# One streaming-encoder layer on one core: norm and weight loads given out a piece ahead of their squares, gate sigmoids a slot behind their loads

## The chip, the cores and the metric

The kernel runs on one core of a Trainium2 chip. The metric is the device time of one execution in microseconds; lower is better. Of the kernel before, three runs and one profiled execution are at hand.

## The reference, cut to what matters

One layer of an encoder for 2048 new frames (16 tiles of 128 rows) and for 8 running streams of 16 frames each (one more tile, number 16, called NT). Two mixers run side by side: differential attention (4 heads) and stick-breaking attention (8 heads of 64, taken in pairs). Their outputs are gated and merged.

```python
h = rms_norm(x, norm_g) * (1.0 + scale) + shift
qa, ka, va, za, qb, kb, vb, zb, ga, gb = split(h @ w_in)
...
s = einsum('bqhcd,bkhcd->bhcqk', qa, ka) * HEAD_DIM_A ** -0.5        # chunk-causal mask
p = softmax(s);  w = p[:, :, 0] - lam * p[:, :, 1];  oa = w @ va
...
z = einsum('bqhd,bkhd->bhqk', qb, kb) * HEAD_DIM_B ** -0.5
log_a = log_sigmoid(z) + cumsum(log_1m, reverse=True) - log_1m;  ob = exp(log_a) @ vb
...
oa = rms_norm(oa, subln_g) * (1.0 - lam_init)
ya = (oa * silu(za)) @ w_branch_a
yb = (ob * silu(zb)) @ w_branch_b
x = x + gate * ((sigmoid(ga) * ya + sigmoid(gb) * yb) @ w_out)
y = rms_norm(x, final_g)
```

The running streams attend to a cache of 512 past frames each (cache_a_k, cache_a_v, cache_b_k, cache_b_v) beside their own frames. Keys and values are returned too.

## The kernel before, in words

Every matmul operand is split in two float16 parts (a high part and what it leaves, three products per matmul), after a scaling by a power of two. The power follows from a bound: the sum of the squares of the weights or cache rows. So each piece of weights and of cache is loaded, squared and summed on ScalarE (`sum_squares`, line 281 is its instruction), and scaled and split later on (`split`, lines 299 to 304).

The program has three stages. In the first (to about 70 us) the modulated inputs are made and stored. The second runs eight units, one head or pair of heads each: even units are differential attention, odd ones stick-breaking. A unit walks over the 17 tiles; `steps` is the list of the 136 pairs of unit and tile. A step projects a tile (lines 438 and 514, running about five tiles ahead), computes scores (lines 649 to 653), turns them into weights on VectorE, ScalarE and GpSimd, has them transposed by DMA (`turn`, line 590, tile wt) and multiplies them with the values two steps later (lines 706 to 711).

Three kinds of side work are dealt out over the steps as lists of small functions called pieces, at the head of each step:

- `prepare_unit` makes the next unit's weights: four pieces `norm` (a load and its square), one `bounds`, four pieces `cut` (the split); odd units the same once more for the gates' weights.
- `norms` returns two lists. `spare` has 48 pieces `one`: a load and its square, for the branch weights, w_out and the cached values. `cached` has 34 pieces `stages` for the 32 pieces of cached keys: a piece splits and stores one, squares the next and loads the one after that.
- The pace is set by the loop over steps: so many pieces per step that a list is through by its due step.

All of these take their 4 KB buffers (wa, wb) from one list, `free`: the front is popped, what is done with is appended. Loads and stores are issued from SyncE's queue (`load` is `nc.sync.dma_start`). Within the engines' queues a scheduler sets the order from the order in which the program is written and from what depends on what.

The third stage (from about 1820 us) is the last phase. Slot n does the branch matmuls of tile n (`branches`, line 1366), the output matmuls of tile n−1 (`output`, line 1395), the rows of tile n−2 (`normed_rows`), and `inputs` of tile n+2: its loads of o, z and the gates' rows (g_d, line 1222), the sigmoid of z, the gates' sigmoids, a sum of squares and the split (line 299, tile hs). `turned` transposes the split tile on TensorE (line 1209). Beside them runs the lane of the cached streams (`sample`, tiles dsc, v16c, dks). Four gate buffers serve two tiles in turn. `act` (line 123) is the helper through which sigmoids and exponentials go, in an order that is kept.

Of the kernel before, what the change touches and what calls it, by code (L numbers as in the profile page):

```python
# [20 lines left out]
AF = mybir.ActivationFunctionType  # L21
# [4 lines left out]
P = 128  # L26
D = 1024
KT = D // P
# [85 lines left out]
def layer_kernel(ctx: ExitStack, tc: tile.TileContext, a: dict):  # L114
# [201 lines left out]
    def prepare_unit(u, keep=None):  # L316


        h, kind = u // 2, u % 2
        U = dict(h=h, kind=kind, u=u, w=[], wg=[], bufs=[])  # L320
        units[u] = U
        raw = {}
        g0, gw = GATES[u]
        gk = 1024 // gw if gw else 0

        def fetch(name, k):
            raw[name, k] = b = free.pop(0) if keep is None else keep[:, k // 2, :]
            if name == "w":
                st = b.rearrange("p (k j n) -> p k j n", k=2, n=P)
                for i in range(2):  # L330
                    load(out=st[:, i, :, :], in_=w_in[:, k + i, :].rearrange("p (j n) -> p j n", n=512)[:, 4 * kind : 4 * kind + 4, h * P : (h + 1) * P])
            else:
                load(out=b.rearrange("p (k n) -> p k n", k=gk), in_=w_in[:, k : k + gk, 4096 + g0 : 4096 + g0 + gw])

        def norm(name, k, i):
            if k == 0:
                U[name + "acc"] = unit.tile([P, 4], F32, tag=name + "acc", name=name + "acc")
            fetch(name, k)
            sum_squares(raw[name, k], 1024, U[name + "acc"][:, i : i + 1])

        def bounds():
            fsq = total(add_up(U["wacc"], 4))
            U["sw"] = scales(fsq, unit, "sw")
            U["fsq"] = unit.tile([P, 1], F32, tag="fsq", name="fsq")
            V.tensor_copy(out=U["fsq"], in_=fsq)

        def bounds_g():
            U["sg"] = scales(total(add_up(U["gacc"], KT // gk)), unit, "sg")

        def split_to(name, k):  # L350

            b = free.pop(0)
            U["bufs"].append(b)
            if keep is None:
                free.append(raw[name, k])
            return raw[name, k], b.bitcast(F16)

        def cut(k):
            st, w = split_to("w", k)
            for i in range(2):  # L360
                x = w.rearrange("p (i f n) -> p i f n", i=2, f=2)[:, i, :, :]
                split(x[:, 0, :], x[:, 1, :], st[:, i * 512 : (i + 1) * 512], U["sw"][:, 0:1], S if i % 2 else G)
                U["w"].append(x)

        def gate_cut(k):
            st, w = split_to("g", k)
            w = w.rearrange("p (k f n) -> p k f n", k=gk, f=2)
            split(w[:, :, 0, :], w[:, :, 1, :], st.rearrange("p (k n) -> p k n", k=gk), U["sg"][:, 0:1], S if k else G)
            U["wg"].append(w)

        pieces = [lambda k=k: norm("w", k, k // 2) for k in range(0, KT, 2)] + [bounds] + [lambda k=k: cut(k) for k in range(0, KT, 2)]
        if gw:
            pieces += [lambda k=k: norm("g", k, k // gk) for k in range(0, KT, gk)] + [bounds_g] + [lambda k=k: gate_cut(k) for k in range(0, KT, gk)]
        return pieces

    def finish_unit(u):
# [460 lines left out]
    def norms():  # L837
# [3 lines left out]
        srcs += [(caches[name][:, i * 8 : i * 8 + 8, h * P : (h + 1) * P], csums[:, cache_column(name, h), i : i + 1], 1.0)  # L841
                 for name in ("av", "bv") for h in range(4) for i in range(4)]

        def one(src, dst, scale):
            st = free.pop(0)
            free.append(st)
            load(out=st if len(src.shape) == 2 else st.rearrange("p (j n) -> p j n", n=P), in_=src)
            sum_squares(st, 1024, dst, scale=scale)

        fetched, squared = [], []  # L850

# [34 lines left out]
            if k < len(todo):  # L886
                fetch(*todo[k])

        return [lambda x=x: one(*x) for x in srcs], [lambda k=k: stages(k) for k in range(len(todo) + 2)]

    steps = [(u, t) for u in range(8) for t in [NT] + list(range(NT))]
    back = []
# [63 lines left out]
    with tc.tile_pool(name="p0", bufs=1) as p0:  # L956
# [154 lines left out]
        minus_b = p0.tile([P, KT], F32, name="minus_b")  # L1111
        V.tensor_scalar(out=minus_b, in0=ab[:, 1, :, 0], scalar1=-1.0, scalar2=None, op0=ALU.mult)
        interleave(normed(0))
        for fn in early[0:4]:
            fn()

        def modulated(g):
# [53 lines left out]
            return [(1.0, lambda n=n: piece(n)) for n in (4, 5)]  # L1171

        interleave(modulated(4))
        interleave([(1.0, fn) for fn in early[4:]], modulated(0), normed(1))
        free.extend(first_x)
        for g in range(1, 4):
            beside = normed(g + 1) if g < 3 else gates()
# [34 lines left out]
    def inputs(t):  # L1212

        o, z = hs[0:2]

        nz = 512 if t < NT else D
        load(out=o, in_=o_d[t])
        load(out=z[:, 0:nz], in_=z_d[t][:, 0:nz])
        gs = []
        for j in range(2):  # L1220
            gs.append(L["g"][(2 * len(begun) + j) % 4].rearrange("p (b n) -> p b n", b=2))
            load(out=gs[j], in_=g_d[t].rearrange("p (b n) -> p b n", b=2)[:, :, j * 512 : (j + 1) * 512])
        begun.append(t)
        r = L["orms"][:, 4 * t : 4 * t + 4] if t < NT else rsqrt(osums[:, NT, :], 4, P, tiny, "rA")
        G.tensor_tensor(out=o[:, 0:nz], in0=o[:, 0:nz], in1=z[:, 0:nz], op=ALU.mult)
        sg = z[:, 512:D] if t < NT else bank("mm")
        act(out=sg, in_=z[:, 0:512], func=AF.Sigmoid)
        for h in range(4):
            c = slice(h * P, (h + 1) * P)
            V.scalar_tensor_tensor(out=o[:, c], in0=sg[:, c], scalar=r[:, h : h + 1], in1=o[:, c], op0=ALU.mult, op1=ALU.mult)  # L1230
        if t == NT:
            sg = bank("mm")
            act(out=sg, in_=z[:, 512:D], func=AF.Sigmoid)
            V.tensor_tensor(out=o[:, 512:D], in0=o[:, 512:D], in1=sg, op=ALU.mult)
        for g in gs:
            act(out=g, in_=g, func=AF.Sigmoid)

        sq = tiny.tile([P, 2], F32, tag="usq", name="usq")
        sum_squares(o, D, sq[:, 0:1])
        V.tensor_tensor(out=sq[:, 1:2], in0=sq[:, 0:1], in1=L["wsq"], op=ALU.mult)  # L1240
        sc = scales(sq, unit, "suy", 2)
        u16 = hs[2].bitcast(F16).rearrange("p (f n) -> p f n", f=2)
        split(u16[:, 0, :], u16[:, 1, :], o, sc[:, 0:1], S)

        f = unit.tile([P, 2], F32, tag="fuy", name="fuy", bufs=4)
        V.tensor_scalar(out=f[:, 0:1], in0=sc[:, 2:3], scalar1=sc[:, 1:2], scalar2=L["s"][0][:, 1:2], op0=ALU.mult, op1=ALU.mult)
        V.tensor_tensor(out=f[:, 1:2], in0=sc[:, 3:4], in1=L["s"][1][:, 1:2], op=ALU.mult)
        return dict(u16=u16, u=L["u"][len(begun) % 2], f=f, g=gs)

    def turned(st):  # L1250

# [23 lines left out]
    def early_work():  # L1275
# [4 lines left out]
        def first(t):  # L1280
            if "orms" not in L:
                L["orms"] = rsqrt(osums[:, 0:NT, :].rearrange("p t h -> p (t h)"), 4 * NT, P, con, "orms")
            states[t] = inputs(t)
            if t == tiles[0]:
                turned(states[t])

        def rest():
            L["g"], L["u"], (L["y"], L["y16"]) = free[0:4], free[4:6], free[6:8]
# [36 lines left out]
    with ExitStack() as c2:  # L1325
# [111 lines left out]
        for n in range(NT + 3):  # L1437
# [5 lines left out]
            if n + 1 <= NT:  # L1443

                work.insert(2, (0.9, lambda n=n: turned(states[tiles[n + 1]])))
            if n > 1:
                work.insert(2, (0.1, lambda n=n: normed_rows(tiles[n - 2], boxes[n - 2])))
            if 0 < n <= NT + 1:
# [31 lines left out]
```

## Time and profile before

| | |
|---|---|
| median of 3 runs | 2332.06 us (2321.65 to 2335.35) |
| profiled execution | 2326.12 us, span 2324.3 us |
| granted TensorE clock, mean | 0.969 |
| busy: TensorE, VectorE, ScalarE, GpSimd | 90%, 75%, 70%, 30% |
| moved by DMA | 445.30 MB, 192 GB/s |
| DMA queue of SyncE | 76.4% of 16 engines' span |

A row of the waits reads: the engine that waited, its tile and line, `<-` what it waited for, then us in total, times and the longest. In the timeline a row is start, duration, engine, line, operation, and in brackets the idle time ahead of it and what ended it. Idle time of an engine costs something only where TensorE, which is busy for most of the span, waits behind it.

### The profile page before, as it was taken

To read this page: it belongs to the slowest core of one execution; us is meant where nothing else is said; L and a number is where in the kernel's file an instruction comes from. 1 tells how busy PE (TensorE), PEld (TensorE's weight loads), DVE (VectorE), ACT (ScalarE), POOL (GpSimd) and SP (SyncE) were. 2 spreads that over 40 slices of the span, in tenths; PEclk is the share of its full clock that TensorE was granted. 3 is DMA by queue.
4 is the path that set the end of the run, shared out by engine and by line. 5 is a ranking of instruction groups with operands and counts; after the bars stand their busy time and mean duration, and the time that the engine had idled before them with its cause. 6 is when DMAs were issued, how large, how long until landed. Compare 5 with 4: busy or idle time off the path is not lost. (4 is left out here: it accounts for less than half of the span.)

```text
span 2324.3 us, 41797 instructions
## 1 busy us (share of the span) xinstructions
PE 2096.5 (90%) x14752; PEld 1123.2 (48%) x14752; DVE 1745.0 (75%) x3795; ACT 1621.7 (70%) x3228; POOL 704.5 (30%) x610
## 2 busy tenths in 40 slices
PE   5998899998989889899998998999998689899998
PEld 3654454444545445455554444555454344444443
DVE  4658668789776777997767879787778878777763
ACT  4968676788776677878676887776677666556541
POOL 1223014356410433752023346401345312122111
PEclk7999999999999999999999999999999799999999
DMA  9778558889696798878877898665667899778421
GB/s 335 272 213 212 134 146 220 198 198 184 174 239 150 201 231 186 187 184 220 183 200 206 182 221 199 171 156 138 142 157 165 191 273 256 211 219 215 143 100 52
DMA packets 805827, 445.30 MB, mean 192 GB/s; under 512 B 537354, under 2 KB 744506, under 8 KB 805104
## 3 DMA queue, kind: packets, MB, share of 16 engines
q1 hardware_dynamic: 804668, 442.24, 76.4%
q8 instruction: 115, 1.88, 0.3%
q14 instruction: 96, 0.79, 0.1%
q10 hardware_dynamic: 948, 0.39, 0.1%
HBM read 228.82 MB, written 86.02 MB: 135 GB/s over the span
## 5 line engine op out<-in xcount | busy, mean ns | idle before, releaser
L632 POOL TENSOR_TENSOR sc_p<-sc_p,sc_n 128x127 f32<-128x127 f32 (+7 forms) x192 | 311.8, 1628 | 660.2 <-DVE sc_n L626 562.8
L438 PEld LDWEIGHTS <-hs 128*128 128x128 f16 x3120 | 276.5, 99 | 263.3 <-issue 11.9
L438 PE MATMUL ps_mm<-wa,hs 128*128 128x512 f16 x1590 | 400.4, 382 | 2.9 <-DMA hs<-hT_d 2.1
L438 PE MATMUL ps_mm<-wb,hs 128*128 128x512 f16 x1530 | 394.5, 384 | 7.6 <-DMA hs<-hT_d 6.8
L626 DVE TENSOR_TENSOR_SCAN sc_n<-ps_s,sc_n,zero_t 128x512 f32<-128x512 f32 x192 | 245.4, 1278 | 72.2 <-ACT ps_s L123 67.3
L649 PE MATMUL ps_s<-k,qst 128*128 128x512 f16 (+3 forms) x640 | 226.0, 354 | 49.2 <-DVE sc_n L626 38.5
L583 DVE TENSOR_TENSOR sc_n<-sc_p,sc_n 128x128 f16<-128x128 f32 (+7 forms) x192 | 222.7, 1163 | 36.8 <-ACT sc_n L582 36.4
L514 PEld LDWEIGHTS <-hs 128*128 128x128 f16 x1632 | 156.5, 98 | 189.1 <-ACT qst L542 5.9
L123 ACT ACTIVATE sc_p<-ps_s,usc 128x512 f32<-128x512 f32 (+3 forms) x320 | 205.1, 641 | 32.5 <-PE ps_s L650 23.3
L650 PE MATMUL ps_s<-k,qst 128*128 128x512 f16 (+3 forms) x640 | 225.7, 354 | 0.0
L514 PE MATMUL ps_t<-wb,hs 128*128 128x512 f16 x918 | 216.1, 379 | 3.0 <-DVE sam L542 1.4
L710 PE MATMUL ps_o<-v,wt 128*128 128x128 f16 x1088 | 168.9, 225 | 43.1 <-DMA wt<-sc_n 42.7
L123 ACT ACTIVATE ps_s<-ps_s,usc 128x512 f32<-128x512 f32 (+3 forms) x328 | 200.5, 611 | 0.0
L582 ACT CAST sc_n<-sc_p 128x128 f16<-128x128 f32 (+7 forms) x192 | 155.2, 811 | 63.7 <-POOL sc_p L632 62.8
L1395 PE MATMUL ps_o<-wo,wb 128*128 128x512 f16 x816 | 185.2, 382 | 6.3 <-ACT wo L299 5.5
L514 PE MATMUL ps_t<-wa,hs 128*128 128x512 f16 x714 | 170.6, 381 | 6.9 <-ACT qst L542 5.7
L710 PEld LDWEIGHTS <-wt 128*128 128x128 f16 x1088 | 105.0, 101 | 104.7 <-DMA wt<-sc_n 54.6
L711 PE MATMUL ps_o<-v,wt 128*128 128x64 f16 x1088 | 154.5, 198 | 0.0
L568 DVE TENSOR_SCALAR_CACHE_REDUCE sc_n<-ps_s,usc 128x512 f32<-128x512 f32 (+3 forms) x160 | 106.2, 664 | 35.2 <-PE ps_s L650 17.2
L1366 PEld LDWEIGHTS <-wb 128*128 128x128 f16 x816 | 79.2, 100 | 105.5 <-issue 23.1
L711 PEld LDWEIGHTS <-wt 128*128 128x128 f16 x1088 | 102.9, 100 | 50.9 <-issue 2.2
L1395 PEld LDWEIGHTS <-wb 128*128 128x128 f16 x816 | 78.7, 98 | 100.4 <-issue 9.1
(370 smaller groups left out, 4515.6 us busy)
## 6 DMA issues: line engine op xcount, KB each, us to landing
hs<-hT_d SPq DMA_DIRECT2D x130, 512.0 KB, 4.6
g_d<-gt SPq DMA_DIRECT2D x68, 256.0 KB, 4.3
out_dram<-pr SPq DMA_DIRECT2D x204, 64.0 KB, 2.2
wa<-g_d SPq DMA_DIRECT2D x25, 512.0 KB, 3.8
o_d<-o SPq DMA_DIRECT2D x136, 64.0 KB, 2.6
hs<-o_d SPq DMA_DIRECT2D x17, 512.0 KB, 3.8
out_dram<-x SPq DMA_DIRECT2D x17, 512.0 KB, 2.8
wide<-in_w_ada_dram SPq DMA_DIRECT2D x8, 1024.0 KB
```

Source lines behind the costliest of these rows:

```text
L123: i = S.activation(**kw)
L438: T.matmul(box["p"], box["h"][:, hi, k, :], U["w"][k][:, wi, :], start=(n == 0), stop=(n == 3 * KT - 1))
L514: T.matmul(box["g"][:, 0:gw], box["h"][:, hi, k, :], U["wg"][k // per][:, k % per, wi, :], start=(j == 0), stop=(j == 3 * KT - 1))
L582: S.copy(out=hi, in_=src)
L583: V.tensor_tensor(out=lo, in0=src, in1=hi, op=ALU.subtract)
L626: V.tensor_tensor_scan(out=dst[:, lo : lo + n][:, ::-1], data0=src[:, 0:n][:, ::-1], data1=zero_t[:, 0:1].to_broadcast([P, n]), initial=fi ...
L632: G.tensor_tensor(out=p[:, 0:m], in0=p[:, 0:m], in1=n[:, 1 : m + 1], op=ALU.mult)
L649: T.matmul(p[:, 0:n], qst[:, c, :], kk[:, c, 0:n], start=True, stop=False)
L650: T.matmul(p[:, 0:n], qst[:, 2 + c, :], kk[:, c, 0:n], start=False, stop=not diag)
L710: T.matmul(po[:, c * P : (c + 1) * P], wt[:, wj, :], vt[:, c, :, :], start=first, stop=False)
L711: T.matmul(po[:, c * P : c * P + 64], wt[:, nb + wj, :], vt[:, c, 0, :], start=False, stop=last)
L1395: T.matmul(po, st["y"][:, yi * 8 + k, :], wo[j * 4 + k // 2][:, wi, k % 2, :], start=(n == 0), stop=(n == 3 * KT - 1))
```

## The change

In `prepare_unit` the load is taken out of `norm`, and a new function `staged` builds the pieces: piece i loads the i-th part and squares the part before it, so that there is one piece more for each list. In `norms` the function `one` does the same with the list `loaded`; a buffer goes back to `free` after its square and not at its load. The first unit's pieces ahead of `modulated` are five and not four, so that they hold the same four loads and squares. In the last phase the gates' sigmoids leave `inputs` for a function `opened`, which the first tile calls behind its `turned` and every other tile one slot after its loads.

```diff
         def norm(name, k, i):
             if k == 0:
                 U[name + "acc"] = unit.tile([P, 4], F32, tag=name + "acc", name=name + "acc")
-            fetch(name, k)
             sum_squares(raw[name, k], 1024, U[name + "acc"][:, i : i + 1])
+
+        def staged(name, ks):
+            def piece(i):
+                if i < len(ks):
+                    fetch(name, ks[i])
+                if i > 0:
+                    norm(name, ks[i - 1], i - 1)
+            return [lambda i=i: piece(i) for i in range(len(ks) + 1)]
...
-        pieces = [lambda k=k: norm("w", k, k // 2) for k in range(0, KT, 2)] + [bounds] + [lambda k=k: cut(k) for k in range(0, KT, 2)]
+        pieces = staged("w", list(range(0, KT, 2))) + [bounds] + [lambda k=k: cut(k) for k in range(0, KT, 2)]
         if gw:
-            pieces += [lambda k=k: norm("g", k, k // gk) for k in range(0, KT, gk)] + [bounds_g] + [lambda k=k: gate_cut(k) for k in range(0, KT, gk)]
+            pieces += staged("g", list(range(0, KT, gk))) + [bounds_g] + [lambda k=k: gate_cut(k) for k in range(0, KT, gk)]
...
-        def one(src, dst, scale):
-            st = free.pop(0)
-            free.append(st)
-            load(out=st if len(src.shape) == 2 else st.rearrange("p (j n) -> p j n", n=P), in_=src)
-            sum_squares(st, 1024, dst, scale=scale)
+        loaded = []
+
+        def one(k):
+            if loaded:
+                st, dst, scale = loaded.pop(0)
+                sum_squares(st, 1024, dst, scale=scale)
+                free.append(st)
+            if k < len(srcs):
+                src, dst, scale = srcs[k]
+                st = free.pop(0)
+                load(out=st if len(src.shape) == 2 else st.rearrange("p (j n) -> p j n", n=P), in_=src)
+                loaded.append((st, dst, scale))
...
-        return [lambda x=x: one(*x) for x in srcs], [lambda k=k: stages(k) for k in range(len(todo) + 2)]
+        return [lambda k=k: one(k) for k in range(len(srcs) + 1)], [lambda k=k: stages(k) for k in range(len(todo) + 2)]
...
-        for fn in early[0:4]:
+        for fn in early[0:5]:
...
-        interleave([(1.0, fn) for fn in early[4:]], modulated(0), normed(1))
+        interleave([(1.0, fn) for fn in early[5:]], modulated(0), normed(1))
...
-        for g in gs:
-            act(out=g, in_=g, func=AF.Sigmoid)
-
...
+    def opened(st):
+
+        for g in st["g"]:
+            act(out=g, in_=g, func=AF.Sigmoid)
...
             if t == tiles[0]:
                 turned(states[t])
+                opened(states[t])
...
                 work.insert(2, (0.9, lambda n=n: turned(states[tiles[n + 1]])))
+                work.append((0.1, lambda n=n: opened(states[tiles[n + 1]])))
```

ScalarE's order in the last phase, from the square of one tile to the cast of the next. wb_1433 and wa_171 are one pair of gate buffers before, wb_1427 and wb_1432 a pair of the change; L123 on them is a sigmoid of the gates, L123 on hs_181 the sigmoid of z, L1372 the cast of the merged branches. Before:

```order
L281 ACTIVATE junk,usq<-hs_180 128x1024
L299 ACTIVATE v16c<-dc,s_c 128x8x128
L1372 CAST wa_173<-wb_1433 128x512
L299 ACTIVATE v16c<-dc,s_c 128x8x128
L281 ACTIVATE junk,facc<-x_23013 128x1024
L299 ACTIVATE hs_182<-hs_180,suy 128x1024
L123 ACTIVATE hs_181<-hs_181 128x512
L299 ACTIVATE v16c<-dc,s_c 128x8x128 x2
L1210 COPY wb_1432<-ps_s 128x1024
L1372 CAST wa_173<-wa_171 128x512
L123 ACTIVATE wb_1433<-wb_1433 128x1024
```

and in the changed kernel (L1389 is the cast, L1224 the copy of the transposed tile):

```order
L281 ACTIVATE junk,usq<-hs_180 128x1024
L281 ACTIVATE junk,facc<-x_23011 128x1024
L299 ACTIVATE hs_182<-hs_180,suy 128x1024
L123 ACTIVATE hs_181<-hs_181 128x512
L123 ACTIVATE wb_1427<-wb_1427 128x1024
L123 ACTIVATE wb_1432<-wb_1432 128x1024
L1389 CAST wa_173<-wb_1426 128x512
L299 ACTIVATE v16c<-dc,s_c 128x8x128 x2
L1224 COPY wb_1428<-ps_s 128x1024 x2
```

Before, a gate's sigmoid stands behind the cast that reads the same buffer for the tile two slots earlier, so its load lies between the two. In the change both sigmoids of a pair stand together behind the sigmoid of z, ahead of the casts of the tile in work.

SyncE's queue in the second unit, where the norms load w_out (L847 before, L861 in the change), beside transposes of weights (L590, L597) and loads of the modulated inputs (L415, L422). Before:

```order
L700 DMA o_d_67<-o 128x128
L847 DMA wa_176<-in_w_out_dram 128x1024
L847 DMA wa_169<-in_w_out_dram 128x1024
L415 DMA hs_182<-hT_d_59 128x2048
L518 DMA g_d_104<-gt_1421 128x512
L847 DMA wa_176<-in_w_out_dram 128x1024
L847 DMA wa_169<-in_w_out_dram 128x1024
L847 DMA wa_176<-in_w_out_dram 128x1024
L590 DMA_TRANSPOSE wt<-sc_n 128x16x128
```

and in the changed kernel:

```order
L597 DMA_TRANSPOSE wt<-sc_n 128x14x128
L861 DMA wb_1432<-in_w_out_dram 128x1024
L597 DMA_TRANSPOSE wt<-sc_n 128x14x128
L889 DMA keys_ak_127<-wa_172 128x2048
L869 DMA wa_176<-in_cache_a_k_dram 128x8x128
L707 DMA o_d_67<-o 128x128
L422 DMA hs_182<-hT_d_59 128x2048
L525 DMA g_d_104<-gt_1421 128x512
L861 DMA wa_172<-in_w_out_dram 128x1024
```

The norms' loads stand farther apart, between the transposes, and the load of the next piece of cached keys (L855 before, L869 now) stands right behind the store of the one before (L875 before, L889 now).

## The prediction

> **What bounds the kernel now.** I read the page first, then the busy times by stretch, then the waits of ScalarE, TensorE and the DMA queue of SyncE, then the timeline where they meet. TensorE carries the span:
>
> ```profile
> PE 2096.5 (90%) x14752; PEld 1123.2 (48%) x14752; DVE 1745.0 (75%) x3795; ACT 1621.7 (70%) x3228; POOL 704.5 (30%) x610
> ```
>
> The whole idle time of TensorE is 2324.3 − 2096.5 = 227.8 us, and a change that only moves loads and ScalarE work can win no more than its part of that. The stretches show where it lies (columns: us, then busy time and count of PE, PEld, DVE, ACT, POOL, the granted clock, the DMA share, GB/s):
>
> ```profile
> 200.00:1770.00 1570.00, 1450.08 (x10188) 784.35 (x10187) 1226.68 (x2575) 1177.24 (x2514) 535.35 (x462) 0.98 0.79 185
> 1770.00:1900.00 130.00, 93.54 (x706) 51.13 (x705) 103.85 (x167) 86.60 (x127) 46.37 (x31) 0.83 0.91 209
> 1900.00:2300.00 400.00, 369.44 (x2685) 180.71 (x2683) 286.18 (x652) 218.56 (x305) 74.81 (x49) 0.98 0.66 184
> 1500.00:1700.00 200.00, 192.46 (x1349) 105.72 (x1347) 153.90 (x351) 134.57 (x300) 42.73 (x38) 0.98 0.63 150
> 1130.00:1330.00 200.00, 183.51 (x1243) 97.82 (x1241) 149.21 (x298) 145.21 (x305) 58.63 (x50) 0.98 0.79 192
> 700.00:900.00 200.00, 185.11 (x1239) 98.44 (x1238) 143.83 (x288) 143.31 (x302) 58.91 (x51) 0.97 0.80 190
> ```
>
> The attention units after 200 us leave 119.9 us idle, the handover to the last phase (1770 to 1900) 36.5 us, the last phase itself (1900 to 2300) 30.6 us. The edits touch all three. What ScalarE itself loses to the loads in question, in the attention units (line 281 is the helper `sum_squares`; us in total, times, longest):
>
> ```profile
> ACT junk L281 <- DMA wb<-in_w_in_dram: 13.8, 8, 3.7
> ACT junk L281 <- DMA wb<-in_cache_a_v_dram: 11.0, 6, 3.4
> ACT junk L281 <- DMA wa<-in_cache_b_k_dram: 9.1, 4, 3.6
> ACT junk L281 <- DMA wa<-in_w_in_dram: 7.0, 3, 2.6
> ACT junk L281 <- DMA wa<-in_cache_b_v_dram: 6.3, 7, 1.9
> ACT junk L281 <- DMA wa<-in_w_out_dram: 5.4, 4, 2.2
> ACT junk L281 <- DMA wa<-in_cache_a_v_dram: 3.7, 2, 3.4
> ACT junk L281 <- DMA wb<-in_cache_b_k_dram: 3.4, 2, 2.2
> ACT junk L281 <- DMA wb<-in_cache_a_k_dram: 3.0, 1, 3.0
> ACT junk L281 <- DMA wb<-in_cache_b_v_dram: 2.9, 1, 2.9
> ACT junk L281 <- DMA wa<-in_cache_a_k_dram: 2.3, 2, 1.4
> ACT junk L281 <- DMA wb<-in_w_branch_a_dram: 1.0, 1, 1.0
> ```
>
> and in the last phase, where line 123 is the helper `act` and g_d the gates' rows:
>
> ```profile
> ACT wa L123 <- DMA wa<-g_d: 50.0, 18, 5.2
> ACT wb L123 <- DMA wb<-g_d: 15.4, 6, 6.7
> ```
>
> So 68.9 us and 65.4 us of ScalarE's time. ScalarE is busy 70% of the span, and its waits count only where TensorE waits behind them.
>
> **The change, part by part.** No instruction is added or taken away; every load, square and sigmoid is there as often as before. What moves is the place.
>
> *The staged loads.* The squares of the key cache already run a piece behind their loads (`stages` squares the buffer of the piece before), so the trace holds the cure beside the complaint. Key rows above (in_cache_a_k, in_cache_b_k): 9.1 + 3.4 + 3.0 + 2.3 = 17.8 us over 32 squares, 0.56 us each. The others, which this change stages: 51.1 us over at most 92 squares (48 norms, 28 pieces of weights, 16 of gate weights), 0.56 us each. A piece of lead has so far bought nothing. One key load shows why:
>
> ```profile
> 782.99 0.39 SPq L855 DMA_DIRECT2D wa<-in_cache_b_k_dram  x1
> 786.90 1.06 ACT L281 ACTIVATE junk<-wa 128x1024 f16<-128x1024 f32 x1 [3.60 <-DMA wa<-in_cache_b_k_dram]
> 787.85 0.29 PE L710 MATMUL ps_o<-v,wt 128*128 128x128 f16 x1 [3.28 <-DMA wt<-sc_n]
> ```
>
> The load leaves SyncE 3.9 us ahead of its square, because its buffer had only just been given back, and ScalarE stands for 3.6 us. What such a stand costs TensorE I take from coincidence. ScalarE's 41 waits (the first and the last of them below) with the 6 us behind each cover 286.5 us of the 1570, and 33.1 us of TensorE's idle time begins inside them; by chance it would be 286.5/1570 × 119.9 = 21.9 us.
>
> ```profile
> 222.52 1.15 ACT L281 ACTIVATE junk<-wb,g 128x1024 f16<-128x1024 f32 x1 [0.96 <-DMA wb<-in_w_branch_a_dram]
> 1366.14 1.06 ACT L281 ACTIVATE junk<-wa 128x1024 f16<-128x1024 f32 x1 [0.18 <-DMA wa<-in_cache_b_v_dram]
> ```
>
> The excess is 11.2 us for all 68.9 us of waits, so 51.1/68.9 × 11.2 = 8.3 us for the staged ones. The key rows say that staging need not remove them, a lead of a whole step of the unit says that most should go; I take half, **−4 us**. Ends: 0 (they wait like the keys) and −33 (all the coincidence is cause).
>
> *The price of staging.* Each preparation has one or two pieces more (10 or 20 where 9 or 18 were) and is still through by the same step, since they are dealt out over the steps left. More weighty: a buffer of the list `free` is now held from load to square. Following the list through the program, the 32 key loads take a buffer given back in the same step 28 times, 20 before; the norms' loads take one given back in the step before 31 times of 48, 9 before. A load into a fresh buffer waits in SyncE's queue for that buffer's reader, and the transposes of line 590, for which TensorE waits, stand behind it:
>
> ```profile
> SPq L590 <- DVE csc L870: 28.6, 10, 4.8
> PE ps_o L710 <- DMA wt<-sc_n: 42.7, 29, 4.9
> ```
>
> The new order, though, puts a key load right behind the key store that awaits the same split, so it adds no wait of its own there; and a norm's buffer given back one step ago has been squared long since. I take 0, with the end of +29 us worked out under the rivals.
>
> The first unit's fifth piece ahead of `modulated` runs the same four loads and squares in the same order: 0.
>
> *The gates' sigmoids.* Before, a sigmoid follows its load by a landing time and blocks what is queued behind it on ScalarE: the evacuations of the cached-stream lane (dsc), the square and the split of the next tile. TensorE feels that where a transposition needs a PSUM bank that the lane's scan (line 626) still reads:
>
> ```profile
> PE ps_s L1209 <- DVE dsc L626: 17.7, 5, 5.7
> ...
> 1922.62 1.06 ACT L123 ACTIVATE wa<-wa 128x1024 f32<-128x1024 f32 x1 [1.79 <-DMA wa<-g_d]
> 1926.69 0.75 PE L1209 MATMUL ps_s<-id,wa 128*128 128x128 f16 x8 [3.91 <-DVE dsc L626]
> ...
> 1976.60 1.06 ACT L123 ACTIVATE wa<-wa 128x1024 f32<-128x1024 f32 x1 [4.89 <-DMA wa<-g_d]
> 1981.57 0.40 PE L806 MATMUL ps_t<-v16c,dwt 128*32 128x256 f16 x8 [0.49 <-DVE v16c L304]
> ...
> 2006.16 1.06 ACT L123 ACTIVATE wa<-wa 128x1024 f32<-128x1024 f32 x1 [3.36 <-DMA wa<-g_d]
> 2010.23 1.07 PE L1209 MATMUL ps_s<-id,wa 128*128 128x128 f16 x16 [1.41 <-DVE dsc L626]
> ...
> 2063.72 1.06 ACT L123 ACTIVATE wa<-wa 128x1024 f32<-128x1024 f32 x1 [5.24 <-DMA wa<-g_d]
> 2066.99 0.29 PE L806 MATMUL ps_t<-v16c,dwt 128*32 128x256 f16 x4 [0.76 <-ACT v16c L299]
> 2069.07 0.40 PE L806 MATMUL ps_t<-v16c,dwt 128*32 128x256 f16 x8 [0.39 <-DVE v16c L304]
> ```
>
> Of each pair the smaller counts: 1.79 + 0.49 + 1.41 + 0.76 + 0.39 = 4.8 us. Behind most of the other gate waits no wait of TensorE follows within 6 us: matmuls of other tiles cover them. **−5 us**; ends 0 and −30.6 (all idle time of 1900 to 2300). A loss is bounded by the order: both sigmoids now stand straight behind the sigmoid of z, before the casts of the tile ahead, so they are done a good part of a slot before the tile that needs them; only at the last tiles could the pair (2 × 1.06 us) come late, +2.1.
>
> The Trainium skill (TensorE: Matmul & The Clock Gate, HAM oscillation) asks that TensorE never idle over about 3.4 us, as its clock then halves. The eight transpositions behind the 3.91 us took 0.75 us; the same rule would add the slower restart of that one wait to the gain, which a granted clock of 0.98 over 1900 to 2300 leaves below a microsecond, so the sum stays.
>
> *The handover.* The split of a w_out piece on ScalarE, for which TensorE waits once, stood behind two gate sigmoids, and now it does not:
>
> ```profile
> 1880.66 1.14 ACT L299 ACTIVATE wo<-x,s_w 128x1024 f16<-128x1024 f32 x1
> 1881.86 3.57 PE L1395 MATMUL ps_o<-wo,wb 128*128 128x512 f16 x8 [5.55 <-ACT wo L299]
> ```
>
> Its own load and the table change ahead of it stay, so **−1 us**; ends −5.5 and 0.
>
> **Sum.** −4 − 5 − 1 = −10 us on the profiled execution's 2326.1 us (span 2324.3 and 1.8 around it): 2316 us. The median of the runs shown, 2332.06, lies 5.9 us above that execution, so I expect a median of **2322 us**. About 1% (23 us) is what a measurement of this kernel can tell from no change, and the forecast is within it.
>
> **Rivals.**
>
> *ScalarE's waits set the pace of the units (faster).* For it: the stretches 700 to 900 and 1130 to 1330 idle 14.9 and 16.5 us of 200, the stretch 1500 to 1700, after the last of these loads, 7.5. The excess of 8.2 us over the 5.7 such stretches between the first and the last of the waits (222 to 1366) is 47 us; if half of it hangs on the waits, 23 us, and the gates bring 10: 2332 − 33 = **2299 us**. Against it: the same stretches also carry the splits and key stores, which stay (GpSimd 58.6 and 58.9 us busy against 42.7), and the coincidence above is weak. The Trainium skill (Perfetto Trace Analysis, Identifying the Most-Contended Engine) calls matmul busy time a poor measure of headroom and points to weight loads, here 48%; that speaks for more slack than 227.8 us and so for this rival, though no row here turns it into time.
>
> *The buffer list runs dry (slower).* The place is SyncE's queue in the units. The count above gives 8 + 22 = 30 more loads with a fresh buffer; at 28.6/10 = 2.9 us each that is 86 us in front of transposes. If a third reaches TensorE, 29 us, less the gates' 5: **2356 us**. It decides from about 28 us of added waits on wt. Against it: of the fresh buffers the norms' are a whole step old, and the transposes mostly wait for their own data.
>
> *The staging does nothing.* The order within the engines is chosen again, squares move up behind the loads as the keys' did, and only the gates count: 2332 − 5 = **2327 us**.
>
> **How the numbers follow.** Forecast 0.47, its own range 2310 to 2334; ScalarE's waits 0.23; the dry list 0.19; nothing from staging 0.11. The range takes in most of both outer rivals, 2294 to 2357. Faster by over 1%: 0.21 of the first rival's 0.23 and 0.02 of the forecast's 0.47, 0.23. Slower by over 1%: 0.17 of the dry list and 0.02 of the forecast, 0.19. Within 1%: the rest, 0.58.
>
> **What the new profile would show.** ScalarE's waits on g_d near zero, the five TensorE waits on the lane's scan (17.7 us) down by 3 to 5 us; L281's waits on loads of norms and weights halved, the key rows unchanged; TensorE's wait of 5.55 us at the handover shorter. It would be wrong if TensorE's idle time from 200 to 1770 moved by more than 15 us either way: downward the first rival, upward, with more on wt, the second.

## The result, and the profile after

The changed kernel takes 2327.91 us (median of 12 runs, 2320.35 to 2333.56), the kernel before 2330.36 us beside it: a ratio of 0.9989, interval 0.9976 to 1.0001, or −2.5 us (−5.6 to +0.2) where −10 was forecast. The profiled execution takes 2323.62 us against 2326.12, span 2321.8, granted clock 0.970 against 0.969. Single executions of one kernel lie up to 14 us apart, so a difference of a few us between one profile of each proves nothing by itself. The clock of 0.970 is the highest of the twelve runs; their mean is 0.965.

The page's busy times, and the busy times by stretch (columns as in the prediction):

```profile
PE 2100.0 (90%) x14752; PEld 1129.4 (49%) x14752; DVE 1732.0 (75%) x3795; ACT 1624.0 (70%) x3228; POOL 689.0 (30%) x610
```

```profile
200.00:1770.00 1570.00, 1450.28 (x10168) 786.65 (x10166) 1221.31 (x2572) 1177.49 (x2511) 527.76 (x461) 0.98 0.78 185
1770.00:1900.00 130.00, 94.21 (x708) 53.64 (x705) 104.35 (x167) 88.50 (x132) 46.07 (x30) 0.83 0.92 212
1900.00:2300.00 400.00, 375.65 (x2724) 182.92 (x2723) 279.68 (x657) 222.33 (x309) 68.20 (x52) 0.99 0.69 186
```

TensorE's idle time is 119.7 us in the units (119.9 before), 35.8 us at the handover (36.5) and 24.35 us in the last phase (30.6). In these two executions all of the gain is in the last phase. The first branch matmul divides the span in two; its row in the timeline (start, duration) before and after:

```profile
1837.41 1.04 PE L1366 MATMUL ps_mm<-wa,wb 128*128 128x512 f16 x2
```

```profile
1840.27 1.03 PE L1383 MATMUL ps_mm<-wb,wa 128*128 128x512 f16 x4
```

Up to it the change is 2.9 us later; from it to the end of the span it takes 2321.8 − 1840.3 = 481.5 us where 2324.3 − 1837.4 = 486.9 were taken, 5.4 us less.

Yet the staged loads did to ScalarE what they were made for. ScalarE's waits after the change (us in total, times, longest):

```profile
ACT hs L123 <- DMA hs<-z_d: 15.3, 5, 5.2
...
ACT wb L123 <- DMA wb<-g_d: 9.5, 3, 4.4
...
ACT junk L281 <- DMA wa<-in_cache_a_k_dram: 7.7, 6, 2.0
ACT junk L281 <- DMA wb<-in_w_in_dram: 7.4, 4, 3.5
ACT junk L281 <- DMA wb<-in_cache_b_v_dram: 5.1, 4, 2.2
ACT wa L299 <- DMA keys_bk<-wa: 4.7, 3, 3.0
ACT junk L281 <- DMA wa<-in_w_out_dram: 4.5, 3, 2.6
...
ACT junk L281 <- DMA wa<-in_cache_a_v_dram: 3.5, 2, 2.2
ACT wb L299 <- DMA keys_ak<-wb: 3.5, 2, 2.2
...
ACT junk L281 <- DMA wa<-in_w_in_dram: 2.9, 3, 1.5
...
ACT wb L299 <- DMA keys_bk<-wb: 1.6, 1, 1.6
ACT junk L281 <- DMA wb<-in_w_out_dram: 1.4, 1, 1.4
...
ACT wa L299 <- DMA keys_ak<-wa: 1.1, 3, 0.5
```

The staged loads hold ScalarE for 7.4 + 5.1 + 4.5 + 3.5 + 2.9 + 1.4 = 24.8 us (51.1 before); with the key rows left out here, all keys come to 16.8 us (17.8). New are the four rows of line 299, 10.9 us in all: splits that wait until a key store has read the buffer they write. In the last phase the gates' waits fell from 65.4 to 9.5 us, and the sigmoid of z, which had hardly waited (1.6 us), now waits 15.3.

### The profile page after: what moved, and what is told of

Its sections match the earlier page's. It is cut to its first block, busy times and chain, and to the rows that moved or that the text cites. A ratio compares the mean times of both kernels' runs of the same rounds, so it can differ in the third digit from the quotient of the medians.

```text
span 2321.8 us, 41788 instructions
## 1 busy us (share of the span) xinstructions
PE 2100.0 (90%) x14752; PEld 1129.4 (49%) x14752; DVE 1732.0 (75%) x3795; ACT 1624.0 (70%) x3228; POOL 689.0 (30%) x610
## 5 line engine op out<-in xcount | busy, mean ns | idle before, releaser
L445 PE MATMUL ps_mm<-wb,hs 128*128 128x512 f16 x1734 | 445.0, 383 | 2.0 <-DMA hs<-hT_d 2.0
L445 PE MATMUL ps_mm<-wa,hs 128*128 128x512 f16 x1386 | 352.0, 383 | 2.0 <-DVE v L304 2.0
L590 DVE TENSOR_TENSOR sc_n<-sc_p,sc_n 128x128 f16<-128x128 f32 (+7 forms) x192 | 215.0, 1125 | 39.4 <-ACT sc_n L589 38.4
L123 ACT ACTIVATE sc_p<-ps_s,usc 128x512 f32<-128x512 f32 (+3 forms) x320 | 203.5, 636 | 37.0 <-PE ps_s L657 27.6
L717 PE MATMUL ps_o<-v,wt 128*128 128x128 f16 x1088 | 176.2, 228 | 45.1 <-DMA wt<-sc_n 44.8
L123 ACT ACTIVATE ps_s<-ps_s,usc 128x512 f32<-128x512 f32 (+3 forms) x328 | 198.8, 606 | 0.0
L1412 PE MATMUL ps_o<-wo,wa 128*128 128x512 f16 x816 | 183.0, 380 | 0.7 <-ACT wa L1224 0.7
L718 PE MATMUL ps_o<-v,wt 128*128 128x64 f16 x1088 | 160.6, 200 | 0.0
L633 DVE TENSOR_TENSOR_SCAN sc_n<-ps_s,zero_t 128x128 f32<-128x128 f32 (+3 forms) x128 | 104.3, 815 | 34.5 <-ACT ps_s L123 33.6
L575 DVE TENSOR_SCALAR_CACHE_REDUCE sc_p<-ps_s,usc 128x512 f32<-128x512 f32 (+3 forms) x160 | 106.2, 664 | 30.9 <-PE ps_s L657 22.8
```

Source lines behind the costliest of these rows:

```text
L123: i = S.activation(**kw)
L445: T.matmul(box["p"], box["h"][:, hi, k, :], U["w"][k][:, wi, :], start=(n == 0), stop=(n == 3 * KT - 1))
L575: V.tensor_scalar(out=dst[:, lo : lo + n], in0=p[:, 0:n], scalar1=sc_pos, scalar2=None, op0=ALU.mult, op1=ALU.max, accum_out=job["mx"][:, ...
L590: V.tensor_tensor(out=lo, in0=src, in1=hi, op=ALU.subtract)
L633: V.tensor_tensor_scan(out=dst[:, lo : lo + n][:, ::-1], data0=src[:, 0:n][:, ::-1], data1=zero_t[:, 0:1].to_broadcast([P, n]), initial=fi ...
L717: T.matmul(po[:, c * P : (c + 1) * P], wt[:, wj, :], vt[:, c, :, :], start=first, stop=False)
```

## The experiments

All ratios are to the kernel before, run on the same chip; on those chips it took 2336 to 2340 us, so times are compared by ratio and traces only within a chip. 0.1% is 2.3 us. Three sets of programs share an order in the units, row by row on every engine up to 1770 us: the kernel before and e1; the changed kernel and e2; n1 and e7.

**e1, the gates alone.** The kernel before, and of the change only `opened`:

```diff
-        for g in gs:
-            act(out=g, in_=g, func=AF.Sigmoid)
...
+                opened(states[t])
...
+                work.append((0.1, lambda n=n: opened(states[tiles[n + 1]])))
```

> Only the gates' sigmoids are moved a slot behind their loads; the loads of norms and weights stay as before. Theory A (the gates alone win, the staged loads give nothing or cost a little): the last phase, from the first branch matmul to the last store, is 5 to 6 us shorter, ratio to before 0.9977, ScalarE's waits on g_d fall from 65 to about 10 us, TensorE's idle time from 1900 to 2300 from 30.6 to about 24 us. Theory B (both halves win a little each): 2 to 3 us shorter, ratio 0.999. Theory C (the 2.5 us are chance, the gates are covered by matmuls of other tiles): ratio 1.000, idle time of the last phase near 30 us.

Measured: 0.9990 (0.9974 to 1.0005), −2.3 us. ScalarE waits 10.4 us for g_d, 20.3 us for z. TensorE idles 28.0 us from 1900 to 2300, which is nearer to theory C's 30 than to theory A's 24; the ratios of all three theories lie in the measured interval, so this run by itself does not choose.

**e2, the loads alone.** The changed kernel with the sigmoids back in `inputs`:

```diff
+        for g in gs:
+            act(out=g, in_=g, func=AF.Sigmoid)
...
-                opened(states[t])
...
-                work.append((0.1, lambda n=n: opened(states[tiles[n + 1]])))
```

> Only the loads of norms and weights are staged; the gates' sigmoids stay behind their loads. Theory A: first branch matmul 2 to 4 us later than before (1837.4), ratio 1.001, ScalarE's waits on these loads halved (51 to about 25 us) and TensorE's idle time from 200 to 1770 still near 120 us. Theory B: ratio 0.999, idle time of the units 117 us or less.

Measured: 1.0018 (1.0006 to 1.0030), +4.2 us. The staged loads hold ScalarE for 24.0 us, splits wait 11.4 us for key stores, as in the whole change, and TensorE idles 120.5 us from 200 to 1770. Both e1 and e2 ran on one chip, and their first branch matmuls, e1's and e2's, show where each differs:

```profile
1844.34 0.61 PE L1369 MATMUL ps_mm<-wa,wb 128*128 128x512 f16 x1
```

```profile
1845.99 1.04 PE L1380 MATMUL ps_mm<-wb,wa 128*128 128x512 f16 x2
```

With staging the units end 1.7 us later; from there to the end e1, with the gates moved, takes 2333.6 − 1844.3 = 489.3 us, e2 2337.4 − 1846.0 = 491.4. The signs are those of the whole change, the gates gain and the loads give some back; but 1.7 and 2.1 us are less than two executions of one kernel differ by. What TensorE does with the time up to the first branch matmul is of more use (the columns of the stretches; the kernel before, the change, e1, e2):

```profile
0.00:1837.41 1837.41, 1659.94 (x11676) 911.67 (x11677) 1404.38 (x3030) 1364.00 (x2875) 612.43 (x547) 0.97 0.79 193
0.00:1840.27 1840.27, 1663.05 (x11676) 917.24 (x11677) 1401.89 (x3029) 1364.69 (x2873) 606.37 (x547) 0.97 0.79 192
0.00:1844.34 1844.34, 1661.33 (x11677) 912.45 (x11678) 1405.06 (x3029) 1362.74 (x2873) 610.02 (x546) 0.97 0.79 192
0.00:1845.99 1845.99, 1666.66 (x11676) 917.93 (x11677) 1401.57 (x3033) 1366.74 (x2874) 605.35 (x547) 0.96 0.79 192
```

With staging TensorE idles no longer there (177.2 us in the change against 177.5 before, 179.3 in e2 against 183.0 in e1). It is busy for longer, by 3.1 and 5.3 us, with the same matmuls.

**e3, no wait at all.** How much can waiting for these loads cost? Here the squares, from unit 1 on, read a column that is always there; the loads are still made. No square reads a loaded buffer any more, so buffers also come free earlier than in the change:

```diff
+    still = ones[:, 0:1].to_broadcast([P, 1024])
...
-            sum_squares(raw[name, k], 1024, U[name + "acc"][:, i : i + 1])
+            sum_squares(raw[name, k] if u == 0 else still, 1024, U[name + "acc"][:, i : i + 1], scale=1.0 if u == 0 else 1 / 32)
...
-            sum_squares(st, 1024, dst, scale=scale)
+            sum_squares(still, 1024, dst, scale=1 / 32 if len(src.shape) == 2 else 1.0)
...
-            sum_squares(fetched[0][0], 1024, acc)
+            sum_squares(still, 1024, acc)
```

> The kernel before, but every square of a norm, a cached key or a unit's weights (units 1 to 7) reads a column that lies in SBUF; the loads are still made. The sums are constants near the true ones, so the scales differ a little. ScalarE can then never wait for such a load: its 68.9 us of waits vanish. Theory A (these waits hardly reach TensorE; coincidence puts 11 us of its idle time on them): 5 to 12 us faster, ratio 0.995 to 0.998. The rival that ScalarE's waits set the pace of the units: 20 us faster or more, ratio 0.991 or less. If nothing of them counts: ratio 1.000.

Measured: 0.9965 (0.9949 to 0.9981), −8.2 us (4.4 to 11.9). None of these squares waits for a load any more, and the units' row reads:

```profile
200.00:1770.00 1570.00, 1456.43 (x10213) 788.92 (x10212) 1256.95 (x2595) 1186.55 (x2526) 548.39 (x465) 0.98 0.79 184
```

113.6 us idle instead of 119.9. So 68.9 us of ScalarE's waits are worth about 8 us of TensorE's time, if the order, which is chosen anew here too, is worth nothing. That ScalarE's waits set the pace of the units is not borne out: the rival needed 23 us. Since the order differs, e3 alone excludes it only if that order is not itself some 15 us slower, nearly as much as the worst order below (n2, +17); the change and e2, with half of the staged loads' waits gone and the units' idle time where it was, speak against it too.

**e4, the shorter list.** The kernel before with one 4 KB buffer held back until the branch weights of the last unit:

```diff
+    held = [free.pop()]
...
+        free.extend(held)
+        held.clear()
```

> The kernel before, with one 4 KB buffer kept out of the list `free` until the last unit's branch weights; no load is staged. This is the suspected cost of staging by itself, since staging holds one buffer more. The rival of the dry list: 5 us slower or more, ratio 1.002 and up, with splits on ScalarE waiting for key stores as in the changed kernel (10.9 us). If the list does not matter: 1.000 within the order's own scatter.

Measured: 1.0057 (1.0041 to 1.0074), +13.3 us. The waits of ScalarE name the same kind of stand that the change brought, on key stores, where the kernel before has none:

```profile
ACT junk L281 <- DMA wb<-in_cache_a_v_dram: 15.1, 5, 5.2
ACT junk L281 <- DMA wa<-in_cache_b_v_dram: 14.0, 5, 4.4
...
ACT wa L299 <- DMA keys_bk<-wa: 6.4, 3, 2.5
...
ACT wa L299 <- DMA keys_ak<-wa: 6.0, 4, 2.6
```

That a buffer fewer makes splits wait for stores is shown, 12.4 us of it. The waits on the loads of norms and weights rose as well, from 51.1 to 85.7 us. What a buffer costs is not shown, as n2 below tells.

**e5 and e6, half of the staging.** The changed kernel, in e5 with the norms' pieces as before, in e6 with the weights' pieces as before:

```diff
 e5
...
-        return [lambda k=k: one(k) for k in range(len(srcs) + 1)], [lambda k=k: stages(k) for k in range(len(todo) + 2)]
+        return [lambda x=x: one(*x) for x in srcs], [lambda k=k: stages(k) for k in range(len(todo) + 2)]
...
 e6
...
-        pieces = staged("w", list(range(0, KT, 2))) + [bounds] + [lambda k=k: cut(k) for k in range(0, KT, 2)]
+        pieces = [lambda k=k: both("w", k, k // 2) for k in range(0, KT, 2)] + [bounds] + [lambda k=k: cut(k) for k in range(0, KT, 2)]
...
```

> The changed kernel with the norms' pieces put back as before: the weights' loads staged, the gates' sigmoids moved. Theory A with the cost in the norms' buffers that are held longer: the splits' new waits for key stores (10.9 us) vanish and the kernel is 6 to 8 us faster than before, ratio 0.997. If the cost lies in the weights' staging or in the order chosen anew: as the changed kernel, ratio 0.999.

> The changed kernel with the weights' pieces put back as before (a load and its square in one piece): norms staged, gates' sigmoids moved. The weights staged without the norms came out 11.7 us slower than before. Theory A1 (the weights' staging is what costs, the norms' staging is harmless): 3 to 8 us faster than before, ratio 0.997 to 0.999. Theory A2 (no part has a cost of its own; each edit makes the order within the engines be chosen anew, which moves the time by several us either way): anywhere from 0.995 to 1.005, and the parts do not add up.

Measured: e5 1.0050 (1.0034 to 1.0066), e6 1.0006 (0.9993 to 1.0019). In e5 no split waits for a key store, and it is the slower one, against what was expected; e6 has 20.0 us of such waits and is the faster. The parts do not add up: e1, with neither half, is 0.9990, the change, with both, 0.9989. Time followed neither the waits on loads nor those on stores, so a third theory was formed (A2 in the texts above): that the order, which the scheduler chooses anew for any edit in the units, moves the time by itself.

**n1, n2, n3: edits that move no load away from its square.** n1 deals the norms' and keys' pieces of a step out ahead of the next unit's weights; n2 and n3 change by 0.05 the number of tiles by which projections run ahead:

```diff
 n1
-            for fn in back[: -(-len(back) // max(1, (W_READY if u else W_READY + 2) - t % NT))]:
-                back.pop(0)()
...
+            for fn in back[: -(-len(back) // max(1, (W_READY if u else W_READY + 2) - t % NT))]:
+                back.pop(0)()
 n2
-LEAD = 5.0
+LEAD = 5.05
 n3
-LEAD = 5.0
+LEAD = 4.95
```

> The kernel before, with the side work of a step written down in the other order: norms and cached keys first, then the next unit's weights. Work, leads and buffers held are the same; only the order is chosen anew. Theory A2: the time moves by 3 to 12 us either way (ratio 0.995 to 1.005), as much as the staging did. Theory A1: within 2 us (0.999 to 1.001).

> The kernel before, with the projections' lead over the scores set to 5.05 tiles and not 5.0: a twentieth of a tile, which is meant to do nothing but let the order be chosen anew. Theory A2: 3 to 12 us either way. Theory A1: within 2 us.

> The kernel before with the projections running 4.95 tiles ahead of the scores in place of 5.0; no load, square or buffer is moved between the pieces. If an order chosen anew moves the time by itself: between -0.5% and +0.8%, of either sign, with ScalarE's waits on loads as before (45 to 55 us for norms and weights). If the lead itself is what counts, the opposite of the +0.71% that a lead of 5.05 cost: 0.993 to 0.996.

Measured: n1 0.9970 (0.9957 to 0.9983), n2 1.0071 (1.0053 to 1.0088), n3 1.0007 (0.9996 to 1.0019). ScalarE's waits on the loads of norms and weights are 58.5, 50.5 and 46.9 us in n1, n2 and n3, the kernel before having 51.1: the fastest of the three has most of them. n3 is not the opposite of n2, so the time does not go with the lead; that 5.05 in itself has a bad effect, through where projections fall, is not excluded by two points. An edit that leaves every load with its square is worth from −7 to +17 us here, up to more than any term of the prediction's sum. The traces of n1 and n2, on one chip, name some of the waits: TensorE idles 224.5 us in n1 and 247.0 in n2, of which 6.5 and 23.2 us are for loads of the modulated inputs (hs of hT_d), 59.7 and 69.2 for transposed weights (wt), 40.8 and 27.0 for sc_n from VectorE.

**e7, e8, e9: the same edits in other orders.** e7 is n1 with the gates moved, e8 is n1 with the whole change, e9 is n2 with the staged loads:

```diff
 e7, e8: n1's swap, and
...
+                opened(states[t])
...
 e8, e9:
...
+        pieces = staged("w", list(range(0, KT, 2))) + [bounds] + [lambda k=k: cut(k) for k in range(0, KT, 2)]
...
 e9:
+LEAD = 5.05
```

> The swapped order of the side work (0.997 alone) with the gates' sigmoids moved as in the change; the order in the units is that of the swapped kernel, row by row, so only the last phase differs. Theory A (the gates bring 3 to 7 us whatever stands ahead of them): ratio 0.994 to 0.996, the fastest kernel so far. If the gates' part was scatter as well: 0.997 or more.

> The whole change (staged loads and moved sigmoids) with the side work in the swapped order. If the staged loads have a value or a cost of their own, it stands against the kernel with the swapped order and the gates alone with the sign it had before (staging 0 to 4 us slower: ratio 0.994 to 0.998). Theory A2 (only the order chosen anew counts): anywhere from 0.992 to 1.004, with ScalarE's waits on the loads at about 25 us all the same.

> The staged loads alone, in the order that a lead of 5.05 tiles gives the projections (the kernel before with that lead alone measured 1.0071 of the kernel before). If staging costs TensorE time by itself, through the buffer held longer: 1.0085 to 1.014, that is 3 to 15 us more, with 8 to 20 us of ScalarE's splits waiting for key stores. If it saves what the prediction put on it: about 1.0055. If only the order chosen anew counts: anything from 0.997 to 1.007, that is, also well below 1.0071. ScalarE's waits on the staged loads 20 to 30 us in each case.

Measured: e7 0.9948 (0.9929 to 0.9967), e8 1.0015 (0.9997 to 1.0033), e9 1.0043 (1.0028 to 1.0058). In e9 the staged loads hold ScalarE for 35.0 us and splits wait 14.3 us for stores; it is faster than n2 all the same, against the theory of a price that staging has by itself. A saving of 4 us would fit it, but not e8, which is 15.7 us slower than e7 (14.1 by their medians, on one chip) and above the range expected of a cost or value of its own; that only the order counts fits both. In e8 the place of the loss can be read in part: TensorE idles 229.0 us against e7's 220.6, and its waits on transposed weights (wt) are 67.0 us against 58.0.

e7 takes 2326.31 us against 2337.65 beside it, and its interval lies wholly below the changed kernel's. Its gates against n1's, in ScalarE's waits (n1 first) and in the last phase:

```profile
ACT wb L123 <- DMA wb<-g_d: 53.1, 18, 7.1
ACT wa L123 <- DMA wa<-g_d: 24.5, 7, 5.1
```

```profile
ACT hs L123 <- DMA hs<-z_d: 19.0, 6, 6.7
...
ACT wa L123 <- DMA wa<-g_d: 5.1, 2, 4.6
...
ACT wb L123 <- DMA wb<-g_d: 4.2, 2, 3.4
```

```profile
1900.00:2300.00 400.00, 371.40 (x2683) 181.01 (x2682) 286.30 (x652) 216.42 (x304) 74.20 (x49) 0.97 0.68 186
```

```profile
1900.00:2300.00 400.00, 373.70 (x2721) 183.59 (x2720) 281.85 (x656) 221.51 (x307) 70.77 (x49) 0.97 0.70 186
```

The last two are n1's and e7's stretch from 1900 to 2300: 28.6 us idle and 26.3. The units of both have the same order.

The pairs that differ in one part of the source alone, by their ratios (an interval of a pair is the two runs' added as independent errors). The two kernels of a gates' pair have the same order in the units; those of a staging pair do not, because staging itself has the order chosen anew:

| part | pair | ratio | us |
|---|---|---|---|
| gates | e1 to the kernel before | 0.9990 ± 0.0016 | −2.3 |
| gates | the change to e2 | 0.9971 ± 0.0017 | −6.8 |
| gates | e7 to n1 | 0.9978 ± 0.0023 | −5.1 |
| staging | e2 to the kernel before | 1.0018 ± 0.0012 | +4.2 |
| staging | the change to e1 | 0.9999 ± 0.0020 | −0.2 |
| staging | e8 to e7 | 1.0067 ± 0.0026 | +15.7 |
| staging | e9 to n2 | 0.9972 ± 0.0023 | −6.5 |

The gates' three pairs agree among themselves, with a mean of −4.7 us (± 2.6); the first of them by itself is not clear of zero. Staging's do not: the first two are the same pair of orders twice, +2 us on average, and the other two lie 22 us apart with different signs.

## Why the prediction was right or wrong

The measured 2327.91 us lies 6 us above the forecast of 2322 and inside its own range of 2310 to 2334. That says little for the mechanism: the range holds the kernel before too. The difference is the better test, and there −10 us lies outside the measured −5.6 to +0.2 us. (The prediction held 23 us to be what a measurement can tell; with twelve runs of each it was about 3.) Its steps fared differently.

**The gates' sigmoids: right in place, and in size within the error.** −5 was predicted; −5.4 us from the first branch matmul on in one execution of each, −4.7 ± 2.6 us by the three pairs. The five waits of TensorE on the lane's scan (17.7 us) became the second of these rows, among TensorE's waits after the change:

```profile
PE ps_s L1223 <- ACT hs L299: 8.4, 2, 4.9
...
PE ps_s L1223 <- DVE dsc L633: 7.8, 4, 3.7
...
PE ps_mm L1383 <- DVE r L262: 6.7, 3, 2.7
```

that is, 7.8 us instead of 17.7, down by 9.9 and not by 3 to 5. Part of that went back into small waits at the branch matmuls, so it is partly luck that the sum came out near the forecast. "Near zero" for the waits on g_d was nearly so (9.5 us); that the load of z would then be the one to wait for (1.6 to 15.3 us) the prediction had not seen. ScalarE's waits on g_d and z fell by 65.4 + 1.6 − 9.5 − 15.3 = 42.2 us, TensorE's idle time by 6.2.

**The handover: the place right, the cure not.** The wait of 5.55 us on wo is gone, as said. But TensorE now stands at the next transposition, for the split of its tile:

```profile
1856.49 0.62 PE L1223 MATMUL ps_s<-id,hs 128*128 128x128 f16 x8 [3.49 <-ACT hs L299]
...
1890.89 0.80 PE L1223 MATMUL ps_s<-id,hs 128*128 128x128 f16 x8 [4.92 <-ACT hs L299]
```

and ScalarE's timeline shows what that split stood behind:

```profile
1879.29 1.13 ACT L299 ACTIVATE wo<-x,s_w 128x1024 f16<-128x1024 f32 x1
...
1884.15 1.28 ACT L123 ACT_TABLE_LOAD   x1
1887.28 0.63 ACT L123 ACTIVATE hs<-hs 128x512 f32<-128x512 f32 x1 [1.85 <-DMA hs<-z_d]
1887.81 1.99 ACT L123 ACTIVATE wb<-wb 128x1024 f32<-128x1024 f32 x2
1889.70 1.13 ACT L299 ACTIVATE hs<-hs,suy 128x1024 f16<-128x1024 f32 x1
```

The split of wo runs early, without a wait. The two sigmoids that no longer stood in front of it now stand in front of the tile's split, together with the table load and the wait for z. The stretch idles 0.7 us less; −1 had been taken, for another reason (the load and the table staying).

The same two waits bear on the clock. Behind the wait of 3.49 us the granted clock (third column from the right) is 0.5 from 1857.0 to 1863.8, behind that of 4.92 us from 1891.2 to 1894.6:

```profile
1857.00:1860.40 3.40, 2.56 (x23) 2.26 (x22) 2.78 (x3) 3.40 (x5) 0.00 (x0) 0.51 0.94 244
1860.40:1863.80 3.40, 3.40 (x12) 1.36 (x11) 1.28 (x1) 0.83 (x1) 1.12 (x1) 0.50 1.09 251
1891.20:1894.60 3.40, 2.88 (x29) 2.62 (x27) 0.95 (x1) 2.33 (x3) 0.00 (x0) 0.50 1.07 222
```

The Trainium skill (TensorE: Matmul & The Clock Gate, HAM oscillation) warns of idle gaps over about 3.4 us; the trace agrees for both waits. In the slow stretch four matmuls of line 1383 take 1.91 us (from 1860.06), behind it eight take 1.89 (from 1863.89). So half of TensorE's busy time in these stretches is 3.0 and 1.4 us: an estimate of the most that the slower clock cost there; the length of the wait does not order the two. The prediction put this cost below a microsecond for the kernel before's wait of 3.91 us; there the clock is 0.51 from 1927.0 to 1930.4 with TensorE busy throughout, which by the same estimate is up to 1.7 us.

**The staged loads: the step that failed.** "I take half, −4 us", with a price of staging of 0. What the step foresaw of ScalarE came out: the waits on the staged loads halved, the key rows stayed. What it derived from that did not: in this order the units end 2.9 us later in the profiled execution, and the pairs give +2 ± 3 us for it. Four things bear on the term.

- *The size of all the waits held.* The coincidence of ScalarE's waits with TensorE's idle time gave 11.2 us for all 68.9 us of waits (14.6 if every idle time that begins inside counts, 36.5 us and not 33.1); e3 measured 8.2 (4.4 to 11.9), with the order's scatter not taken out. The Trainium skill (Perfetto Trace Analysis, Optimization Strategy) has one start from the gaps of the engine that one wants faster and go back to what blocks them; by e3 this case agrees, since of a neighbour's 68.9 us only about 8.2 were TensorE's.
- *ScalarE's price was not 0.* A buffer held from load to square leaves one fewer for the rest, and of the 26.3 us that ScalarE won, 10.9 came back as waits for key stores. That these waits cost TensorE time is not shown: its idle time did not rise. The prediction looked for the price in SyncE's queue, ahead of the transposes; in this order little of it is there (the rows below), in e8 against e7 9.0 us.
- *TensorE was busy for longer, not idle.* Up to the first branch matmul it idles no longer with staging, but is busy for 3.1 and 5.3 us more. Over all runs the mean granted clock is lower with staging: 0.963 in e2 against 0.968 in e1 and in the 31 runs of the kernel before, all on one chip; 0.965 in the twelve runs of the change. A slower clock would fit the longer busy time, and it has no term in the sum. It is not shown as the cause: the busy times of two executions with one order differ by 1.4 us (the kernel before and e1) and 3.6 us (the change and e2), the clock was not varied by itself, and n2, the slowest order, has 0.967.
- *The term is smaller than what it rides on.* Any edit in the units makes the scheduler choose the order anew, and three such edits that stage nothing were worth −0.30%, +0.07% and +0.71%. In three orders staging measured +2, +16 and −6.5 us. The sum gave this scatter no term; the forecast's own range of −22 to +2 us around 2332 would have had to reach some 17 us to the slow side for it alone.

TensorE's waits on transposed weights read before the change:

```profile
PE ps_o L710 <- DMA wt<-sc_n: 42.7, 29, 4.9
...
PE ps_o L706 <- DMA wt<-sc_n: 20.8, 19, 2.6
```

and after it:

```profile
PE ps_o L717 <- DMA wt<-sc_n: 44.8, 28, 4.3
...
PE ps_o L713 <- DMA wt<-sc_n: 22.0, 16, 2.8
```

That is 3.3 us more, where the rival was to be decided from about 28 us.

So the rival of the dry list did not come to pass as told, though its cause, the shorter list, did.

What stays open: whether staging has a value of its own. Four pairs in three orders cannot tell it from 0; and why n1's order takes about 23 us less than n2's with the same work was not found, though the rows above name some of the waits that differ. The e4 run, +0.57%, is no larger than n2's +0.71% and does not settle the price of a buffer either.

**Which rivals fell.** ScalarE's waits as the pace of the units, by the units' idle time, which did not move, and by e3 within the order's scatter. The dry list as the prediction told it, by the wt rows. "Only the gates count" gave 2327 us, and the measured 2327.91 is nearest to it; by the pairs its sum describes this order best, with staging at +2 ± 3 us. Its reason does not: the squares were to move up behind their loads, but the waits on those loads halved. It had 0.11.

## What to carry to other kernels

Before an idle time of one engine is worth something, follow it to the engine that bounds the kernel: waits of 68.9 us were worth about 8.2, and the five rows where two waits met came near the gates' gain. Where a scheduler chooses the order anew for every edit, measure a few edits that should do nothing first; a term smaller than their scatter is read only from pairs whose order is otherwise the same, and a reordering (here n1's swap with the gates moved, 0.9948) may be worth more than the edit. A load staged ahead holds its buffer longer, so look for the wait among the next users of the list, not only among the next loads. Read the granted clock over all runs, and busy time beside idle time: the profiled execution had the highest clock of its kernel's twelve.

## What the runs showed of the hardware that was not expected

Behind a wait of 3.49 us TensorE was granted half its clock for 6.8 us, behind one of 4.92 us for 3.4 us: the shorter wait had the longer slow stretch. No row here tells why. Not of the hardware but of the order: that a lead of 5.05 tiles in place of 5.00 costs 0.71%, with the same work and nearly the same waits of ScalarE on loads (50.5 us against 51.1), and 4.95 nothing clear (1.0007), was not expected in its size.
